# Dilated attention of the later queries: distant keys by residue class instead of densely

## Chip, core and metric

The kernel runs on one core of a Trainium2 chip, in one launch. The metric is the device time of the whole launch in microseconds, the median of the runs. Engines are named as the profile names them: PE (TensorE), PEld (its weight loads), DVE (VectorE), ACT (ScalarE), POOL (GpSimd) and SP, which issues the DMAs.

## What is computed

One decoder layer of 1024 tokens and width 1024: an input projection feeds eight heads of dilated attention (width 64 each) and four heads of a gated linear recurrence (HGRN2); both are normalised, joined by `w_out`, and followed by a squared-ReLU MLP. What matters here is the attention. It mixes three causal patterns, weighted by their softmax denominators:

```python
DILATED_PATTERNS = ((128, 1), (512, 4), (2048, 16))   # (window, dilation)
...
span = window // dilation
valid = (dist >= 0) & (dist <= span) & (blk * ATTN_BLOCK + kj - ATTN_BLOCK >= 0)
bias = -slopes[:, None, None] * (dist * dilation).astype(jnp.float32)
...
w = jax.nn.softmax(jnp.stack(lses, axis=0), axis=0)
o = jnp.sum(w[..., None] * jnp.stack(outs, axis=0), axis=0)
```

The mixture equals one softmax in which a key counts once for each pattern that holds it. A query at distance d sees every key with d <= 128, every key with d a multiple of 4 up to 512, and every key with d a multiple of 16. Beyond 128 tokens only keys of the query's own residue class modulo 4 can count.

## The kernel before

The stages follow one another: input normalisation and first projection, the recurrence heads (`hgrn_core`, four times), the attention, the output projection, the MLP. All matmuls are fp32; most operands are split into a high and a low part (`split_into`, `three_pass`), so that one product is two or three matmuls. The order on every engine is the order of the program (`manual_schedule`): each engine runs its instructions in the order in which they are written, and waits between engines are put in by data dependence. SP, too, issues its DMAs in that order, and waits in that order.

The attention works with blocks of 128 queries. For head `hd` and block `b` there is one step, 64 in all:

- `score` multiplies the block's queries with all keys up to the block's own end, `(b + 1) * 128` of them, in pieces of at most 512, once for the high and once for the low part of the keys. DVE adds the bias table (which holds the logarithm of the count, the ALiBi slope, and -1e30 where no pattern holds the key) and takes the maximum in the same instruction (L738).
- `expo` takes the exponential on ACT with the sum as by-product (L749).
- `turn` transposes the 128 x 128 blocks of the result on PE (L762), and ACT and DVE split them (L765, L766).
- `weigh` multiplies with the values for two blocks of queries at a time (`g = b // 2`, L779). The queries' high and low value halves come out as two halves of 64 rows.
- `finish` transposes back (L790), adds the halves (L794), and POOL multiplies by the reciprocal of the sums (L795).

The loop runs a pipeline by hand: in step s it issues the exponentials of step s + 1, the scores of step s + 2, the transposes of step s, the weighing of the pair of blocks before, and `finish` of the one before that. After these it takes work from `queue`, a list of generators (`fill`). A generator yields after each unit of about three matmuls. In the attention stage the queue holds the projections of the next pair of heads (`attn_proj`: 16 units each for queries, values and keys, 48 a pair), and later the first half of the output projection (`early_out`). `UNITS` says how many units follow each step; in the last 20 steps a budget of about 1000 ns does. `hooks` places single pieces of work, such as weight loads (`w_get`), at given steps.

`attn_proj` writes queries and keys of two heads into stacks and lets DMAs copy halves between partitions (L620, L621, L651, L652); `keys_off` and `keys_late` do this for the keys. `load_bias` loads one head's bias table of 1024 columns (L715). Tiles come from pools with tags: P (3 slots), S and T (9 each), BT and V8 (2 each), and PSUM banks `mm`, `s`, `t` and `pv` (2 each). A new tile waits for the readers of the one that held its slot.

Of the kernel before, what the change touches and what calls it, by code (L numbers as in the profile page):

```python
# [17 lines left out]
P = 128  # L18
# [9 lines left out]
LEVELS = (1, 2, 4, 8, 16, 32, 64)  # L28

# [6 lines left out]
def hymba_layer(ctx, tc, x, w_in, w_out, w_ff1, w_ff2, g_pre, lb_logits, g_mix, g_post,  # L36
# [406 lines left out]
    def hgrn_core(h, scale, after=None):  # L443
# [13 lines left out]
        if h < HH - 1:  # L457
            fill(1200 * scale)
            totals = slab("P", f"tot{h}")
            for step in range(3):  # L460
# [43 lines left out]
                cur = nx  # L504
                fill((7000, 7000, 7000)[step] * scale)
# [94 lines left out]
    pairs = [None] * (AH // 2)  # L600
    first_done = [False] * (AH // 2)
# [25 lines left out]

    def keys_early_read():
        pr, stacks, src, hf, _ = put_off.pop()
        put_off.append((pr, stacks, keys_read(pr, src, hf), hf, True))  # L630

    def attn_proj(pr):
# [79 lines left out]
    def load_bias(hd):  # L712
        if hd < AH and hd not in bts:
            bts[hd] = slab("BT", f"bt{hd}") if hd < AH - 1 else early["table"][:, 0]
            nc.sync.dma_start(out=bts[hd], in_=bias_tab[hd])  # L715

    def score(hd, b):
        stacks, _ = pairs[hd // 2]
        if b == 0:
            load_bias(hd)  # L720
            if hd + 1 < AH - 1:
                load_bias(hd + 1)
            stats[hd] = {n: tp.tile([P, NT, 2] if n == "mx" else [P, NT], F32, tag=n, name=f"{n}{hd}", bufs=2)
                         for n in ("mx", "nm", "dn", "rd")}
        q, kh, kl = (stacks[hd % 2][n] for n in ("q", "kh", "kl"))
        nk = (b + 1) * P
        mx, nm = stats[hd]["mx"], stats[hd]["nm"]
        pe = slab("P", f"p{hd}_{b}")
        pieces = []
        qs = q[:, b * P:(b + 1) * P]  # L730
        for pc in range(1 if nk <= 512 else 2):
            k0 = pc * 512
            n = min(512, nk - k0)
            pS = bank("s", f"ps{hd}_{b}_{pc}")
            TE.matmul(pS[:, :n], qs, kh[:, k0:k0 + n], start=True, stop=False)  # L735
            TE.matmul(pS[:, :n], qs, kl[:, k0:k0 + n], start=False, stop=True)  # L736
            o = 896 - b * P + k0
            V.tensor_tensor_reduce(out=pe[:, k0:k0 + n], in0=pS[:, :n], in1=bts[hd][:, o:o + n], scale=1.0,  # L738
                                   scalar=-3.0e38, op0=ALU.add, op1=ALU.max, accum_out=mx[:, b, pc:pc + 1])
            pieces.append((k0, n))  # L740
        if len(pieces) == 1:
            V.tensor_scalar(nm[:, b:b + 1], mx[:, b, 0:1], -1.0, None, op0=ALU.mult)  # L742
        else:
            V.tensor_scalar(nm[:, b:b + 1], mx[:, b, 0:1], mx[:, b, 1:2], -1.0, op0=ALU.max, op1=ALU.mult)
        return pe, nk

    def expo(hd, b, pe, nk):
        nm, dn = stats[hd]["nm"], stats[hd]["dn"]
        S.activation(pe[:, :nk], pe[:, :nk], AF.Exp, bias=nm[:, b:b + 1], accum_out=dn[:, b:b + 1])  # L749
        return pe  # L750

    def turn(hd, b, pe):
        g, u = divmod(b, 2)
        if u == 0:
            ns = (2 * g + 5) // 4
            pts[hd, g] = [[slab("T", f"pt{q}{hd}_{g}_{s}", F32R, (P, 4, 256)) for q in "hl"] for s in range(ns)]
        for s in range((b + 4) // 4):
            nj = min(4, b + 1 - 4 * s)
            pt = bank("t", f"pt{hd}_{b}_{s}")
            for j in range(nj):  # L760
                jj = s * 4 + j
                TE.transpose(pt[:, j * P:(j + 1) * P], pe[:, jj * P:(jj + 1) * P], ident)  # L762
            src = pt[:, :nj * P].rearrange("p (j c) -> p j c", j=nj)
            hi, lo = (q[:, :nj, u * P:(u + 1) * P] for q in pts[hd, g][s])
            S.activation(hi, src, AF.Copy)  # L765
            V.tensor_tensor(out=lo, in0=src, in1=f32(hi), op=ALU.subtract)  # L766
        dn, rd = stats[hd]["dn"], stats[hd]["rd"]
        V.reciprocal(rd[:, b:b + 1], dn[:, b:b + 1])

    def weigh(hd, g):  # L770
        _, vs = pairs[hd // 2]
        pt = pts.pop((hd, g))
        po = bank("pv", f"pov{hd}_{g}")
        nj = 2 * g + 2
        for j in range(nj):
            c0 = P if j == nj - 1 else 0
            vst = vs[:, j, hd % 2].rearrange("p a d -> p (a d)")
            for q in range(2):
                TE.matmul(po[:, c0:256], vst, pt[j // 4][q][:, j % 4, c0:],  # L779
                          start=j == 0 and q == 0, stop=j == nj - 1 and q == 1)  # L780
        ot = sp.tile([P, 256], F32, tag="ot", name=f"ot{hd}_{g}", bufs=1)
        S.activation(ot, po[:, :256], AF.Copy)
        return po, ot

    def finish(hd, g, po, ot):
        pr = hd // 2
        if anats[pr] is None:
            anats[pr] = slab("T", f"anat{pr}", F32, (P, NT, 2, 64))
        for u in range(2):
            TE.transpose(po[:, 256 + u * P:256 + (u + 1) * P], ot[:, u * P:(u + 1) * P], ident)  # L790
        pair = po[:, 256:].rearrange("p (u a d) -> p u a d", u=2, a=2)
        b = slice(2 * g, 2 * g + 2)
        dst = anats[pr][:, b, hd % 2]
        V.tensor_reduce(dst, pair.rearrange("p u a d -> p u d a"), axis=AX.X, op=ALU.add)  # L794
        G.tensor_tensor(out=dst, in0=dst, in1=stats[hd]["rd"][:, b].unsqueeze(2).to_broadcast([P, 2, 64]),  # L795
                        op=ALU.mult)
        if hd % 2 and g == NT // 2 - 1 and pr < AH // 2 - 1:
# [201 lines left out]
    steps = [(hd, b) for hd in range(AH) for b in range(NT)]  # L999
    scored, exped = {}, {}  # L1000

    def look(s):
        if s < len(steps):
            scored[s] = score(*steps[s])

    def raise_(s):
        if s < len(steps):
            exped[s] = expo(*steps[s], *scored.pop(s))

# [3 lines left out]
    def open_attention():  # L1013
        look(0)
        raise_(0)
        look(1)

    for h in range(HH):
# [11 lines left out]
        45: lambda: [drain(), keys_early_read(), row_turn(0, 0, tag="mm"), w_get(WO0 + 1, 0), row_rec(1)],  # L1030
        46: lambda: [keys_late(), early_sums(), queue.extend(early_out(t) for t in range(NE))],
# [13 lines left out]
    UNITS = ((3, 3, 3, 3, 2, 3, 1, 2), (4, 4, 4, 3, 2, 3, 1, 2), (4, 4, 4, 4, 3, 3, 2, 2))  # L1045
    n_steps = len(steps)
    to_weigh, to_fold = [], []
    for s in range(n_steps):
        if s % 16 == 6:
            first_done[s // 16] = True  # L1050
        hd, b = steps[s]
        ready, to_weigh = to_weigh, []
        raise_(s + 1)
        fresh = (s + 2) % 16 == 0
        if not fresh:
            look(s + 2)
        turn(hd, b, exped.pop(s))
        if b % 2:
            to_weigh.append((hd, b // 2))
        to_fold, last_fold = [(i, g, weigh(i, g)) for i, g in ready], to_fold  # L1060
        if fresh and s + 2 < n_steps:
# [927 lines left out]
```

## Time and profile before

| | |
|---|---|
| Median of 3 runs | 1231.17 us (1231.1 to 1232.23) |
| Span of the profiled execution (first to last instruction) | 1229.3 us |
| PE busy | 1220.1 us, 99% |
| DVE busy | 869.4 us, 71% |
| ACT busy | 546.9 us, 44% |
| POOL busy | 308.7 us, 25% |
| DMA, mean over the span | 130 GB/s, 38.5% of 16 engines for the main queue |
| First scores and last weighing of the attention | 302.3 us and 535.6 us |

The profile has no time of its own for the profiled execution beyond its span; the span is 1.9 us below the median of the runs. PE, PEld, DVE, ACT and POOL are engines; "busy" counts the time in which an instruction runs. Because matmuls are pipelined, a busy PE need not be at its peak: the distance between the starts of two matmuls says what one costs. A line such as L762 is a line of the kernel before. A row of groups reads: line, engine, operation, output<-inputs, shapes, count | busy us, mean ns | idle time before, and what ended it.

### The profile page before, as it was taken

The page shows a single profiled execution, that of the slowest core. Times are in us where ns is not written, and L with a number is a line of the kernel's source. Part 1 is how long each engine was busy: PE and PEld are TensorE (multiplying, and loading weights), DVE is VectorE, ACT ScalarE, POOL GpSimd, SP SyncE. Part 2 cuts the span into 40 slices and gives each one's busy share as a digit, 9 for nine tenths or more (in the row PEclk, how much of TensorE's full clock was granted, in tenths as well). Part 3 has the DMA queues.
Part 4 walks back from the last instruction along what each step waited for, and adds up shares of the span by engine and source line. Part 5 has one row for each costly group of instructions (what it writes and reads, how often), then busy time and mean ns, then how long its engine had stood idle before and what let it go on. Part 6 is the DMA issues. An engine that isn't in the chain of part 4 may idle for free.

```text
span 1229.3 us, 17165 instructions
## 1 busy us (share of the span) xinstructions
PE 1220.1 (99%) x6462; PEld 1047.5 (85%) x6462; DVE 869.4 (71%) x1498; ACT 546.9 (44%) x1003; POOL 308.7 (25%) x304
## 2 busy tenths in 40 slices
PE   9999999999999999999999999999999999999998
PEld 8898989888888888888888888888888888888886
DVE  5686969675766667768679667676678555488796
ACT  7633333223565557665575122222244353534562
POOL 0000000012222223246250676756622000000023
PEclk9999999999999999999999999999999999999999
DMA  5201111133232324254334446544487634433337
GB/s 215 70 18 52 35 52 35 35 86 86 70 88 67 86 69 140 78 196 145 117 125 146 171 180 223 194 183 164 153 311 273 238 103 154 155 103 88 119 102 275
DMA packets 61138, 159.75 MB, mean 130 GB/s; under 512 B 5248, under 2 KB 13184, under 8 KB 61056
## 3 DMA queue, kind: packets, MB, share of 16 engines
q1 hardware_dynamic: 61056, 158.66, 38.5%
q8 instruction: 51, 0.84, 0.3%
q14 instruction: 31, 0.25, 0.1%
HBM read 110.40 MB, written 41.94 MB: 124 GB/s over the span
## 4 chain that ended last, share of the span: by engine, by line
PE 96%; ACT 1%; DVE 1%; issue 0%; DMA 0%; POOL 0%; SPq 0%; DVEq 0%; POOLq 0%; ACTq 0%
PE f L1729 18%; PE f2s L1729 7%; PE pov L779 3%; PE pt L762 3%; PE pig L88 2%; PE pig L89 2%; PE pig L87 2%; PE pl L468 2%; PE pwo L87 2%; PE pwo L89 2%; PE pwo L88 2%; PE ps L736 1%; PE ps L735 1%; PE pm_av L87 1%; PE pm_ak L87 1%; PE pm_aq L87 1%
## 5 line engine op out<-in xcount | busy, mean ns | idle before, releaser
L84 DVE TENSOR_TENSOR al<-ar,ah 128x1024 fp32r<-128x1024 f32 x56 | 70.6, 1261 | 80.0 <-ACT ah L83 77.8
L1729 PE MATMUL f<-bh,ah 128*128 128x512 f32 x320 | 124.5, 389 | 0.0
L1729 PE MATMUL f<-bl,ah 128*128 128x512 f32 x320 | 124.5, 389 | 0.0
L1729 PE MATMUL f<-bh,al 128*128 128x512 f32 x320 | 124.5, 389 | 0.0
L83 ACT ACTIVATE ah<-ar 128x1024 fp32r<-128x1024 f32 x56 | 59.1, 1056 | 85.4 <-DMA ar<-actd 85.1
L1729 PEld LDWEIGHTS f<-bl,ah 128*128 128x128 f32 x320 | 60.1, 188 | 12.6
L1729 PEld LDWEIGHTS f<-bh,ah 128*128 128x128 f32 x320 | 60.1, 188 | 12.5
L1729 PEld LDWEIGHTS f<-bh,al 128*128 128x128 f32 x320 | 60.1, 188 | 12.3
L1803 POOL TENSOR_SCALAR lbl<-ssq 128x1 f32<-128x1 f32 x4 | 3.3, 821 | 245.7 <-ACT fd L1799 245.5
L766 DVE TENSOR_TENSOR ptl<-pt,pth 128x512 fp32r<-128x512 f32 (+2 forms) x96 | 50.3, 552 | 20.0 <-ACT pth L765 19.9
L765 ACT ACTIVATE pth<-pt 128x512 fp32r<-128x512 f32 (+2 forms) x96 | 43.3, 486 | 39.4 <-PE pt L762 38.1
L738 DVE CUSTOM_DVE_ANT_0 p<-ps,bt 128x512 f32<-128x512 f32 (+2 forms) x84 | 44.4, 554 | 21.8 <-PE ps L736 21.3
L1352 POOL TENSOR_TENSOR e<-x,e 128x512 f32<-128x512 f32 x14 | 21.6, 1543 | 131.0 <-DVE x L1303 131.0
L795 POOL TENSOR_TENSOR anat<-anat,rd 128x128 f32<-128x128 f32 x32 | 16.3, 510 | 147.2 <-DVE anat L794 144.9
L749 ACT ACTIVATE p<-p,nm 128x128 f32<-128x128 f32 (+3 forms) x64 | 49.5, 773 | 6.4 <-DVE nm L742 6.0
L79 POOL TENSOR_SCALAR ms<-hss 128x8 f32<-128x8 f32 x4 | 0.8, 198 | 199.3 <-DVE hss L585 199.3
L1729 PE MATMUL f2s<-bh,al 128*128 128x512 f32 (+1 forms) x128 | 48.9, 382 | 0.0
L1729 PE MATMUL f2s<-bl,ah 128*128 128x512 f32 (+1 forms) x128 | 48.9, 382 | 0.0
L1729 PE MATMUL f2s<-bh,ah 128*128 128x512 f32 (+1 forms) x128 | 48.9, 382 | 0.0
L762 PE MATMUL pt<-ident,p 128*128 128x128 f32 x288 | 42.5, 274 | 0.3 <-DVE ptl L766 0.3
L84 DVE TENSOR_TENSOR bl<-br,bh 128x1024 fp32r<-128x1024 f32 x32 | 40.1, 1253 | 1.0 <-ACT bh L83 0.9
L779 PE MATMUL pov<-pth,v 128*128 128x256 f32 (+1 forms) x160 | 40.3, 287 | 0.0
(1645 smaller groups left out, 3936.3 us busy)
## 6 DMA issues: line engine op xcount, KB each, us to landing
ar<-actd SPq DMA_DIRECT2D x56, 512.0 KB, 3.7
br<-in_w_ff_dram SPq DMA_DIRECT2D x16, 1024.0 KB, 6.2
w1r<-in_w_ff_dram SPq DMA_DIRECT2D x14, 1024.0 KB, 6.4
raw<-in_w_in_dram SPq DMA_DIRECT2D x26, 512.0 KB, 3.6
actd<-e SPq DMA_DIRECT2D x17, 768.0 KB, 4.1
actd<-e SPq DMA_DIRECT2D x11, 1024.0 KB, 4.0
raw<-in_w_out_dram SPq DMA_DIRECT2D x8, 512.0 KB, 3.5
xres<-in_x_dram SPq DMA_DIRECT2D x8, 512.0 KB, 4.2
```

Source lines behind the costliest of these rows:

```text
L83: S.activation(hi, src, AF.Copy)
L84: eng.tensor_tensor(out=lo, in0=src, in1=f32(hi), op=ALU.subtract)
L87: TE.matmul(dst, lhs[0], rhs[0], start=start, stop=False)
L88: TE.matmul(dst, lhs[0], rhs[1], start=False, stop=False)
L89: TE.matmul(dst, lhs[1], rhs[0], start=False, stop=stop)
L738: V.tensor_tensor_reduce(out=pe[:, k0:k0 + n], in0=pS[:, :n], in1=bts[hd][:, o:o + n], scale=1.0, scalar=-3.0e38, op0=ALU.add, op1=ALU.max ...
L749: S.activation(pe[:, :nk], pe[:, :nk], AF.Exp, bias=nm[:, b:b + 1], accum_out=dn[:, b:b + 1])
L762: TE.transpose(pt[:, j * P:(j + 1) * P], pe[:, jj * P:(jj + 1) * P], ident)
L765: S.activation(hi, src, AF.Copy)
L766: V.tensor_tensor(out=lo, in0=src, in1=f32(hi), op=ALU.subtract)
L779: TE.matmul(po[:, c0:256], vst, pt[j // 4][q][:, j % 4, c0:], start=j == 0 and q == 0, stop=j == nj - 1 and q == 1)
L1729: TE.matmul(pm, a[:, j, c], b[:, j, d], start=start and j == 0 and q == 0, stop=stop and j == 1 and q == 2, skip_group_check=True)
```

## The change

Queries 0 to 511 (blocks 0 to 3) are computed as before and are now called kind D ("dense"). For queries 512 to 1023 the keys are divided in two:

- Kind N ("near"): for blocks 4 to 7 the own block and the one before, 256 keys, densely.
- Kind F ("far"): keys two or more blocks back. The 512 queries are taken by residue class modulo 4, four groups of 128, and each group meets only the 192 keys of its class among tokens 0 to 767. The far bias is -1e30 where a key is less than two blocks back.

A softmax over near and far keys needs a common maximum and a common sum. The near statistics lie by block (partition = token within the block), the far ones by class (partition = token divided by 4). They are brought into each other's order through small DRAM tiles (`swap_dram`): `send` writes 128 x 4 numbers and `receive` reads them in the other order. `joint` takes the larger of the two maxima. Three such exchanges are made per head: near maxima, far maxima, far sums.

Each head now has eight items: D0 to D3, F0, F1 (two classes each), N0, N1 (two blocks each). Far weighing uses values in the class's order, and near weighing adds to the same PSUM bank, which is laid out by class. For this, `attn_proj` writes a pair's values to DRAM, and `far_load` reads them back in rows of 96 keys. The far bias tables are made once during the first three recurrence heads: `far_table` reads every fourth row of each head's bias table, POOL picks every fourth column, and a DMA stores the result (`far_dram`). `load_bias` loads 512 columns of the old table and 192 of the far one.

The order of the loop is written out anew (`ITEMS`, `LOOKS`, `UNITS`), `keys_late` is called once per pair, at step 13 of 16, and the next pair's projections are queued at step 14 of 16.

The core of the diff (allocation of tiles, and bodies that only carry over the old code to kind D, are cut):

```diff
+DIL = 4
+FAR = 192
+FC = FAR // 2
...
                 cur = nx
+                far_table()
                 fill((7000, 7000, 7000)[step] * scale)
...
+    def far_load(pr):
+        fars[pr] = []
+        for c in range(2):
+            t = slab("T", f"vf{pr}_{c}", F32R, (P, DIL, 2, 2, 64))
+            nc.sync.dma_start(out=f32(t[:FC]).rearrange("p r h a d -> p (r h a d)"),
+                              in_=v_dram[pr][c * FC * DIL:(c + 1) * FC * DIL].rearrange("(k r) c -> k (r c)", r=DIL))
+            fars[pr].append(t)
...
+    def far_table():
...
+        for b in range(4, NT):
+            w = (b - 1) * P
+            g = slice((b - 4) * 32, (b - 3) * 32)
+            nc.sync.dma_start(out=raw[g, :w],
+                              in_=bias_tab[hd].rearrange("(i r) c -> i r c", r=DIL)[:, 0, 896 - b * P:896 - b * P + w])
+        G.tensor_copy(far_box["out"][:, hd % 4],
+                      raw[:, :FAR * DIL].rearrange("p (k r) -> p k r", r=DIL)[:, :, 0])
...
+                if n == 6 and hf == 0:
+                    nc.sync.dma_start(out=v_dram[pr].rearrange("(n p) c -> p n c", p=P),
+                                      in_=f32(vs).rearrange("p n h a d -> p n (h a d)"))
+                    if pr == 0:
+                        far_load(0)
...
+    def look(hd, kind, g):
...
+        if kind == "D":
+            b = g
+            jobs = [(q[:, b * P:(b + 1) * P], lambda k: k[:, :(b + 1) * P], st["D"][b], bt[:, 384 - b * P:512], b)]
+        elif kind == "N":
+            jobs = [(q[:, b * P:(b + 1) * P], lambda k, b=b: k[:, (b - 1) * P:(b + 1) * P], st["N"][:, b - 4],
+                     bt[:, 256:512], b) for b in range(4 + 2 * g, 6 + 2 * g)]
         else:
+            jobs = [(q.rearrange("p (m r) -> p r m", r=DIL)[:, r, P:], lambda k, r=r:
+                     k.rearrange("p (m r) -> p r m", r=DIL)[:, r, :FAR], st["F"][:, r], bt[:, 512:512 + FAR], 8 + r)
+                    for r in range(2 * g, 2 * g + 2)]
+        o = 0
+        for qs, keys, dst, bias, i in jobs:
+            n = dst.shape[-1]
+            TE.matmul(pS[:, o:o + n], qs, keys(kh), start=True, stop=False)
+            TE.matmul(pS[:, o:o + n], qs, keys(kl), start=False, stop=True)
+            V.tensor_tensor_reduce(out=dst, in0=pS[:, o:o + n], in1=bias, scale=1.0,
+                                   scalar=-3.0e38, op0=ALU.add, op1=ALU.max, accum_out=mx[:, i:i + 1])
+            o += n
...
+    def tokens(ap, far):
+        flat_ = ap.rearrange("m r -> (m r)")
+        return flat_.rearrange("(m r) -> m r", r=DIL) if far else flat_.rearrange("(b p) -> p b", p=P)
+
+    def send(hd, i):
+        st = stats[hd]
+        src, far = ((st["mx"][:, 8:12], True), (st["mx"][:, 4:8], False), (st["dn"][:, 8:12], True))[i]
+        nc.sync.dma_start(out=tokens(swap_dram[hd][i], far), in_=src)
+
+    def receive(hd, i):
+        dst, far = ((stats[hd]["xf"], False), (stats[hd]["xn"], True), (stats[hd]["xd"], False))[i]
+        nc.sync.dma_start(out=dst, in_=tokens(swap_dram[hd][i], far))
+
+    def joint(hd, i):
+        st = stats[hd]
+        sl, other = ((slice(4, 8), "xf"), (slice(8, 12), "xn"))[i]
+        V.tensor_tensor(out=st["nm"][:, sl], in0=st["mx"][:, sl], in1=st[other], op=ALU.max)
+        V.tensor_scalar(st["nm"][:, sl], st["nm"][:, sl], -1.0, None, op0=ALU.mult)
...
+            for r in range(2 * g, 2 * g + 2):
+                for c in range(2):
+                    for q in range(2):
+                        TE.matmul(po[:, r], v_of(fars[hd // 2][c], r)[:FC], pt[q][:FC, 2 * r + c],
+                                  start=r == 0 and c == 0 and q == 0, stop=False, skip_group_check=True)
+            return None
+        po = stats[hd]["po"].rearrange("p (r m) -> p r m", r=DIL)
+        for j, s0, n, c0 in (((3, 0, 1, 0), (4, 1, 2, 0)), ((5, 3, 2, 1), (6, 5, 2, 2), (7, 7, 1, 3)))[g]:
             for q in range(2):
+                TE.matmul(po[:, :, c0 * 32:(c0 + n) * 32], v_of(vs, j),
+                          pt[q][:, :, s0:s0 + n].rearrange("p r s i -> p r (s i)"),
+                          start=False, stop=j == 7 and q == 1, skip_group_check=True)
...
-    UNITS = ((3, 3, 3, 3, 2, 3, 1, 2), (4, 4, 4, 3, 2, 3, 1, 2), (4, 4, 4, 4, 3, 3, 2, 2))
+    UNITS = ((2, 3, 4, 3, 2, 2, 2, 2), (3, 3, 4, 4, 3, 2, 2, 2), (3, 4, 4, 4, 3, 2, 3, 3))
+    ITEMS = (("D", 0), ("D", 1), ("D", 2), ("D", 3), ("F", 0), ("F", 1), ("N", 0), ("N", 1))
+    LOOKS = {0: ((0, "D", 2), (0, "N", 1)), 1: ((0, "D", 3), (0, "F", 0)), 2: ((0, "F", 1),),
+             6: ((1, "D", 0),), 7: ((1, "D", 1),)}
...
+        if i in (3, 5):
+            joint(hd, 1 if i == 3 else 0)
+        raise_(*((hd, *ITEMS[i + 1]) if i < 7 else (hd + 1, *ITEMS[0])))
+        if s % 16 == 13 and s < n_steps - 16:
+            while not put_off:
                 fill(1.0)
+            keys_late()
...
+        if i == 0:
+            send(hd, 1)
+        elif i == 1:
+            receive(hd, 1)
+        elif i == 2:
+            send(hd, 0)
+        elif i == 3:
+            receive(hd, 0)
+        elif i == 5:
+            send(hd, 2)
+        elif i == 6:
+            receive(hd, 2)
+        if s % 16 == 15 and s < n_steps - 1:
+            far_load(s // 16 + 1)
...
+        if i == 7:
+            look(hd + 1, "N", 0)
```

In this loop `look` issues scores and maxima, `raise_` exponentials, `turn` transposes and splits, `weigh` and `finish` the rest, for one item each. The diff changes nothing in the recurrence's own arithmetic, the output projection or the MLP.

More of the change, by code (lines that the diff above doesn't have):

```diff
@@ L1048, in hymba_layer @@
     for s in range(n_steps):
[L1049 removed]
+        hd, i = divmod(s, 8)
+        if s % 16 == 3:
             first_done[s // 16] = True
[L1051 removed]
         ready, to_weigh = to_weigh, []
[L1053 to L1061, printed above, removed]
[L1062 to L1067 removed]
```

254 lines of the change are left out of this document (153 added, 101 removed).

## The prediction

> **What bounds the kernel now.** I read the page first, then the stretches of the attention stage, then the waits, and last the chain and TensorE's timeline, which give the prices.
>
> ```profile
> span 1229.3 us, 17165 instructions
> ...
> PE 1220.1 (99%) x6462; PEld 1047.5 (85%) x6462; DVE 869.4 (71%) x1498; ACT 546.9 (44%) x1003; POOL 308.7 (25%) x304
> ...
> PE 96%; ACT 1%; DVE 1%; issue 0%; DMA 0%; POOL 0%; SPq 0%; DVEq 0%; POOLq 0%; ACTq 0%
> ...
> 299.80:512.00 212.20, 212.20 (x1288) 186.54 (x1287) 146.07 (x452) 125.83 (x282) 51.75 (x58) 1.00 0.33 93
> 512.00:540.00 28.00, 27.71 (x170) 23.79 (x169) 20.46 (x53) 20.36 (x47) 8.91 (x18) 1.00 0.23 67
> ...
> PE pt L762 <- DVE ptl L766: 0.3, 1, 0.3
> ```
>
> The two long rows are the attention stage: length, then busy time of PE, weight loads, DVE, ACT and POOL, the granted clock, the share of the DMA engines and GB/s. TensorE never stops (212.20 of 212.20 us) and has its full clock (1.00); VectorE works 69% of the time and ScalarE 59%. Its largest wait in this stage is 0.3 us, and 96% of the chain is TensorE. So the stage is as long as the sum of TensorE's instructions, counted from one start to the next (a record's own duration overlaps the next). Work taken from TensorE shortens the kernel one to one while the queue of projection matmuls is filled into the same steps. What DVE and ACT save is worth nothing; what they lose in waiting counts once TensorE runs out of cover.
>
> The span is 1229.3 us and the median of the three runs 1231.17, so 1.9 us lie outside the instructions or between executions. I subtract from the span and carry the 1.9 us along.
>
> **TensorE's prices.** One head now, blocks 4 to 7 (chain, then timeline: start, duration, instruction):
>
> ```profile
> 376.99 0.55 PE pt L762 x5
> ...
> 380.79 0.66 PE pt L762 x6
> 383.90 0.79 PE pt L762 x7
> 384.69 1.38 PE pov L779 x12
> ...
> 387.05 0.88 PE pt L762 x8
> 389.98 1.86 PE pov L779 x16
> ...
> 430.20 0.39 PE L735 MATMUL ps<-kh,q 128*128 128x512 f32 x1
> ...
> 430.65 0.22 PE L735 MATMUL ps<-kh,q 128*128 128x128 f32 x1
> ...
> 430.82 0.52 PE L762 MATMUL pt<-ident,p 128*128 128x128 f32 x3
> ...
> 434.84 0.28 PE L735 MATMUL ps<-kh,q 128*128 128x256 f32 x1
> ...
> 435.07 0.60 PE L762 MATMUL pt<-ident,p 128*128 128x128 f32 x4
> ...
> 438.92 0.33 PE L735 MATMUL ps<-kh,q 128*128 128x384 f32 x1
> ...
> 439.26 0.71 PE L762 MATMUL pt<-ident,p 128*128 128x128 f32 x5
> ```
>
> A pair of score matmuls (kh, kl) costs 0.45 us for 512 keys (430.20 to 430.65), 0.17 for 128, 0.23 for 256 and 0.34 for 384. A transpose costs 0.11 (0.88 / 8), a weighing matmul over 256 queries 0.116 (1.86 / 16). The 128-wide pair is two matmuls of 0.085, but eight transposes in a row, also 128 wide and each with its own weight load, cost 0.11 each; in a long run of short matmuls I take 0.11.
>
> Removed per head (blocks 4 to 7, keys up to the own block):
> - scores: four pairs of 512 and one each of 128, 256, 384 and 512: 4 x 0.45 + 1.19 = 2.99 us
> - transposes, 26: 0.55 + 0.66 + 0.79 + 0.88 = 2.88 us
> - weighing (g = 2, 3): 1.38 + 1.86 = 3.24 us
>
> Together 9.11 us.
>
> Added per head:
> - near scores (kind N), four pairs of 256: 4 x 0.23 = 0.92 us
> - far scores (F), four residues, pairs of 192 keys: between the 128 and the 256 pair; I take two of 0.11, so 4 x 0.22 = 0.88 us
> - transposes, 8 near and 8 far: 16 x 0.11 = 1.76 us
> - far weighing, 16 matmuls 128 wide: 0.085 to 0.11 each, 1.36 to 1.76; I take 1.76 us
> - near weighing, six of 256 and four of 128: 6 x 0.116 + 4 x 0.085 = 1.04 us
>
> Together 6.36 us. The eight transposes of the results stay. Saved: 9.11 - 6.36 = 2.75 us per head, **22.0 us for eight heads**. Blocks 0 to 3 (kind D) keep their instructions. The queued projection work is the same 48 units a pair, only dealt out differently (UNITS), so nothing moves in the sum.
>
> **The price no row shows.** Far queries and keys are read with one fp32 in four, 16 bytes apart. Nearest rows: the first and last of the seven levels of the recurrence (eight products of 64 queries, 16 records):
>
> ```profile
> 253.59 1.89 PE L529 MATMUL pl<-qt,kt 128*128 128x64 f32 x16
> 255.29 0.48 PE L87 MATMUL pm_aq<-hTh,wh 128*128 128x512 f32 x1
> ...
> 283.76 1.89 PE L529 MATMUL pl<-qt,kt 128*128 128x64 f32 x16
> 285.46 0.48 PE L87 MATMUL pm_ak<-hTh,wh 128*128 128x512 f32 x1
> ```
>
> The first reads every second fp32, the last 64 in a row, and both take 1.70 us. So a stride of 8 bytes is free for the moving operand here. For 16 bytes, and for weights, I take free too, because it is nearest to these rows. The other end is four times the price: a weight load of 4 x 0.11 us for each of eight matmuls is 3.5 us instead of 0.88, 2.6 per head, 21 us in all, which would eat the saving. Cheaper than contiguous is excluded, since no fewer elements are read. [...]
>
> **What hides the rest.** VectorE and ScalarE:
>
> ```profile
> L766 DVE TENSOR_TENSOR ptl<-pt,pth 128x512 fp32r<-128x512 f32 x48 | 32.4, 689 | 15.5 <-ACT pth L765 15.4
> ...
> L738 DVE CUSTOM_DVE_ANT_0 p<-ps,bt 128x512 f32<-128x512 f32 x42 | 28.4, 688 | 16.5 <-PE ps L736 16.1
> ...
> L738 DVE CUSTOM_DVE_ANT_0 p<-ps,bt 128x256 f32<-128x256 f32 x14 | 5.9, 420 | 2.5 <-PE ps L736 2.5
> ```
>
> Blocks 4 to 7 now need eight biased maxima and eight splits a head, four of each at 512. After, there are four maxima at 256 (0.42 us each), four at 192 (below that) and four splits at 512 (0.69): VectorE loses some 3 us a head and gains about 1 us of tiny joint operations. ScalarE trades four wide exponentials for eight narrow ones and copies half as much. Neither becomes the bound at 69% and 59%.
>
> The far table (40 small DMAs and eight POOL copies, most of a microsecond each) lies in the first three recurrence heads. POOL's later rsqrt is queued behind these copies, but POOL has little else there. The v spill (1 MB) and its reload (0.8 MB) per pair are read five steps later. I cost these at nothing; if a load lands late, the first far weighing waits and TensorE with it, a few us per pair at most.
>
> **The new wait.** Per head three statistics go out to DRAM and back in token order. `joint` waits on two of them, VectorE first; behind it are queued the split for the next weighing, and on ScalarE the far or near exponentials. Rows for small transfers (KB each, median us from issue to landing; then SP's waits in us, times, longest) and for the stage's length:
>
> ```profile
> q<-ql SPq DMA_DIRECT2D x16, 128.0 KB, 2.2
> ...
> gpre<-in_g_pre_dram SPq DMA_DIRECT2D x1, 4.0 KB, 2.6
> ...
> lbl<-in_lb_logits_dram SPq DMA_DIRECT2D x1, 4.0 KB, 8.9
> ...
> SPq L651 <- POOL ql L650: 31.3, 8, 6.7
> ...
> L735 PEld LDWEIGHTS ps<-kh,q x96: 186/188/192, 302.3 to 522.3; 128*128 128x128 f32 x96
> ```
>
> Scores of step 0 begin at 302.3 and those of step 61 at about 522, 3.6 us a step; minus 22 / 64 that leaves 3.3. The near maxima are ready some 2.8 us into step 0 (scores after the weighing, then the maxima); `joint` for the far half stands at the head of step 3, so out and back have about 3 x 3.3 - 2.8 = 7 us, those of the far maxima 8 us. Two legs at 2.6 us are 5.2 us and fit; 4-byte pieces on one leg may add a microsecond. TensorE has its fill units as cover. Costs arise where a leg queues behind a big load or behind SP's wait for POOL, and in the last two heads, where fill is thinner and steps shorter (about 2.5 us). At 2.2 us a leg the 16 joints cost nothing; at 8.9 they cost far more than the saving. Nearest are the 2.2 and 2.6 rows. My estimate is 0.3 us of TensorE idle for each of 12 joints and 0.6 for the four of the last two heads, **6 us**.
>
> Sum: 1229.3 - 22.0 + 6.0 = 1213.3 us of span, 1215 us with the 1.9.
>
> **Rivals.**
> 1. The exchange binds. SP runs in order: a `receive` waits for its `send`, and both stand behind weight loads and query copies, which SP has waited up to 6.7 us for (row above). If out and back take 9.5 us instead of 5.2, each joint is 2.5 us late and all 16 cost 40 us: 1231 - 22 + 40 = 1249 us, slower. It decides from 22 / 16 = 1.4 us of TensorE idle per joint. For it: TensorE's queue is in order and the last heads have little fill. Against: DMA is 33% busy in this stage, and 16 copies of 128 KB land in 2.2 us.
> [...]
> 3. The change doesn't shorten TensorE's work, since fill takes its place: 1231 us. This needs the chain to be bound by VectorE or by latency instead; 96% PE speaks against it.
> 4. Short matmuls pack better and the exchange is free: far weighing 1.36 instead of 1.76 us a head and no idle, 1231 - 25 = 1206 us.
>
> **How the numbers follow.** Forecast case (1208 to 1222): 0.60. The exchange binding, slower: 0.18. The stride costing: 0.14, of which 0.12 stays faster and 0.02 doesn't. No change: 0.04. Better than forecast: 0.04. A difference of 0.2% (2.5 us) is about what a measurement of this kernel can tell from none. Faster: 0.60 + 0.12 + 0.04 = 0.76; same: 0.04; slower: 0.18 + 0.02 = 0.20. The likeliest case gives 1215. The range runs from 1206 (rival 4) to 1236 (the upper end of the stride); some 0.15 of the exchange's 0.18 lies above it and little below.
>
> **What would show it.** Right: in the attention stage TensorE still full but 16 us shorter, pairs of far scores starting 0.22 us apart, PE transposes 26 a head, and the waits of DVE for the exchanged maxima long without a wait of PE behind them. The exchange is to blame if PE waits on splits or exponentials for over 1.4 us at joints; the stride, if a far pair takes 0.4 us or more at full clock. I am wrong altogether if PE has no idle time and the stage isn't shorter, or if the time is lost outside 300 to 540 us, say by late tables or weights.

## The result

The kernel after takes 1294.8 us (median of 4, 1290.2 to 1298.6) against 1231.1 before on the same chip: 1.0514 times the time, 95% interval 1.0485 to 1.0543. Forecast were 1215 us and 1206 to 1236. The sign was wrong, and the time lies beyond the rival that was to make the kernel slower (1249).

The page of the kernel after, with the lines that answer to those of before:

```profile
span 1290.0 us, 17087 instructions
...
PE 1233.7 (96%) x6366; PEld 1047.0 (81%) x6366; DVE 844.8 (65%) x1426; ACT 534.7 (41%) x1027; POOL 310.9 (24%) x305
...
PE 84%; DMA 8%; DVE 4%; ACT 3%; issue 1%; SPq 0%; POOL 0%; DVEq 0%; POOLq 0%; ACTq 0%
```

The 96 instructions that should go from TensorE went. But DMA holds 8% of the chain that ended last, where it held none. The stretches of the attention stage (columns as before; the second is a piece of the first):

```profile
299.80:575.00 275.20, 231.78 (x1251) 192.40 (x1251) 128.36 (x411) 117.49 (x308) 50.74 (x52) 0.97 0.41 88
540.00:560.00 20.00, 12.73 (x75) 11.20 (x74) 6.29 (x19) 8.44 (x27) 0.80 (x2) 0.83 0.39 116
```

TensorE, full in this stage before, is idle for 43 of 275 us, and its clock is below 1.00 for a part of it. Four periods of 3.4 or 6.8 us at half clock add up to 20.5 us; before there was none.

For a sum I took each TensorE instruction from its start to the next start, set aside gaps above 30 ns as idle, and added up by what the instruction works on, over the whole execution (us). The sums lie 7.6 to 8.1 below the spans in every column, so the columns can be compared. The last row leaves out the fall of the clock at the very end of every execution:

| | before | after | e1 | e6 | e7 | e4 | e12 |
|---|---|---|---|---|---|---|---|
| scores | 34.7 | 43.7 | 35.1 | 34.6 | 34.6 | 26.5 | 30.6 |
| transposes | 29.4 | 24.3 | 25.7 | 21.8 | 20.7 | 19.9 | 19.8 |
| weighing | 38.7 | 42.8 | 48.3 | 41.1 | 39.8 | 38.9 | 38.5 |
| folds of the results | 4.6 | 5.9 | 5.9 | 5.9 | 5.8 | 5.7 | 5.7 |
| projections | 229.9 | 230.6 | 235.9 | 229.1 | 229.9 | 228.9 | 228.8 |
| output product | 96.5 | 99.6 | 99.6 | 98.3 | 97.8 | 96.6 | 96.6 |
| the rest | 786.0 | 786.7 | 786.5 | 786.4 | 785.5 | 786.1 | 786.9 |
| idle | 1.8 | 48.4 | 43.1 | 15.8 | 8.1 | 8.7 | 6.6 |
| at half clock | 0 | 20.5 | 64.9 | 10.2 | 10.2 | 0 | 0 |

Each column is one profiled execution; for e4 and for e12 it is the quickest of the kernel's, at a mean granted clock of 0.999, and the slowest of either had 0.995, which in e10 goes with 10.2 us at half clock, so the zeros need not hold for their medians.

Two things stand out in the column of after: 46.6 us more idle time, and scores that cost 9.0 us more instead of 9.5 less. Three causes can be seen.

**The exchange.** The chain in the stage (start, duration, what), at the first head and at the third:

```profile
311.56 0.42 DVE pn L799
312.02 9.73 DMA swd<-stat
321.81 4.04 DMA stat<-swd
325.94 0.44 DVE stat L821
326.63 0.33 issue
326.97 0.62 ACT pf L835 x3
...
378.07 11.40 DMA swd<-stat
389.53 4.56 DMA stat<-swd
```

From the last near maximum (311.56) to the joint one (325.94) pass 14 us. 9.73 of them is the near maxima's way to DRAM. Over the eight heads this send takes 8.7 to 11.4 us. It writes 512 pieces of 4 bytes, because a partition's four statistics belong to four blocks. Who waits (us in total, times, longest; SP first, then the joint and the exponentials behind it):

```profile
SPq L816 <- DMA swd<-stat: 76.4, 19, 9.9
...
DVE stat L821 <- DMA stat<-swd: 32.3, 6, 7.2
...
ACT pf L835 <- DVE stat L822: 29.2, 7, 6.9
```

**The order inside a look.** TensorE's waits in the same view:

```profile
PE ps_F L797 <- DVE stat L799: 12.2, 16, 1.2
PE ps_N L797 <- DVE stat L799: 10.6, 16, 2.1
PE pt_F L856 <- DVE ptl L865: 7.3, 1, 7.3
PE pt_F L856 <- ACT pf L835: 5.2, 4, 2.9
```

All 32 near and far looks make TensorE wait in their middle, 22.8 us together. The timeline of one of them (start, duration, instruction, idle before it):

```profile
381.35 0.34 DVE L799 CUSTOM_DVE_ANT_0 pf<-ps_F,bt 128x192 f32<-128x192 f32 x1
381.61 0.08 DVE L799 DVE_READ_ACCUMULATOR2_ANT stat<- 128x1 f32 x1
381.74 0.31 PEld L797 LDWEIGHTS ps_F<-kh,q 128*128 128x128 f32 x1 [1.15 <-DVE stat L799]
381.75 0.55 PE L797 MATMUL ps_F<-kh,q 128*128 128x192 f32 x1 [0.91 <-DVE stat L799]
...
382.11 0.42 PE L798 MATMUL ps_F<-kl,q 128*128 128x192 f32 x1
...
382.35 0.62 PE L920 MATMUL pov_far<-ident,pn 128*128 128x128 f32 x4
```

The loop in `look` issues a job's two matmuls and its maximum, then the second job's into the other columns of the same PSUM tile, and the second job's matmul waits on VectorE's semaphore for the first job's maximum. Before, a piece had a bank of its own. Here two groups share one, and the 32 waits last 0.71 us on the average.

**The stride.** The pair that follows the wait takes 0.60 us (381.75 to 382.35) where 0.22 was assumed, and its weight load 0.31 us instead of the 188 ns of before. A part of the 0.60 belongs to the wait: in e7 below, without the wait, the 32 far pairs take 15.4 us, 0.48 each.

### The profile page after: what moved, and what is told of

The parts are those of the page before. It is cut to its first block, busy times and chain, and to the rows that moved or that the text cites. A ratio compares the mean times of both kernels' runs of the same rounds, so it can differ in the third digit from the quotient of the medians.

```text
span 1290.0 us, 17087 instructions
## 1 busy us (share of the span) xinstructions
PE 1233.7 (96%) x6366; PEld 1047.0 (81%) x6366; DVE 844.8 (65%) x1426; ACT 534.7 (41%) x1027; POOL 310.9 (24%) x305
## 4 chain that ended last, share of the span: by engine, by line
PE 84%; DMA 8%; DVE 4%; ACT 3%; issue 1%; SPq 0%; POOL 0%; DVEq 0%; POOLq 0%; ACTq 0%
PE f L1870 17%; PE f2s L1870 7%; DMA swd<-stat 4%; DMA stat<-swd 2%; PE pig L92 2%; PE pig L90 2%; PE pig L91 2%; PE pl L471 2%; PE pwo L90 2%; PE pwo L91 2%; PE pwo L92 2%; PE pm_f L90 1%; PE pm_f L92 1%; PE pm_f L91 1%; PE pm_ak L90 1%
## 5 line engine op out<-in xcount | busy, mean ns | idle before, releaser
L1870 PEld LDWEIGHTS f<-bh,ah 128*128 128x128 f32 x320 | 60.1, 188 | 12.5
L925 POOL TENSOR_TENSOR anat<-anat,stat 128x128 f32<-128x128 f32 (+1 forms) x24 | 13.1, 544 | 183.8 <-DVE anat L924 165.0
L1887 ACT ACTIVATE acc<-f 128x512 f32<-128x512 f32 x28 | 16.8, 598 | 49.1 <-PE f L1870 49.1
L86 ACT ACTIVATE bh<-br 128x1024 fp32r<-128x1024 f32 x32 | 33.6, 1051 | 4.6 <-PE f L1870 2.9
L87 DVE TENSOR_TENSOR wl<-raw,wh 128x1024 fp32r<-128x1024 f32 x23 | 29.0, 1263 | 9.1 <-ACT wh L86 8.5
L864 ACT ACTIVATE pth<-pt_D 128x128 fp32r<-128x128 f32 (+3 forms) x32 | 13.8, 432 | 50.3 <-PE pt_D L845 50.3
L658 POOL TENSOR_TENSOR kl<-kf,kh 64x512 fp32r<-64x512 f32 x16 | 20.4, 1275 | 50.7 <-ACT kh L657 50.1
L865 DVE TENSOR_TENSOR ptFl<-pt_F,ptFh 96x512 fp32r<-96x512 f32 x16 | 11.0, 687 | 32.1 <-ACT ptFh L864 31.1
L90 PE MATMUL pwo<-woh,mt 128*128 128x512 f32 x80 | 31.6, 395 | 0.3 <-ACT esum L1032 0.3
```

The lines of the kernel that those rows point to most:

```text
L87: eng.tensor_tensor(out=lo, in0=src, in1=f32(hi), op=ALU.subtract)
L90: TE.matmul(dst, lhs[0], rhs[0], start=start, stop=False)
L658: G.tensor_tensor(out=stacks[i]["kl"][a:b, sl], in0=full[a:b], in1=f32(stacks[i]["kh"][a:b, sl]), op=ALU.subtract)
L925: G.tensor_tensor(out=dst, in0=dst, in1=st["rd"][:, b].unsqueeze(2).to_broadcast([P, n, 64]), op=ALU.mult)
L1870: TE.matmul(pm, a[:, j, c], b[:, j, d], start=start and j == 0 and q == 0, stop=stop and j == 1 and q == 2, skip_group_check=True)
L1887: S.activation(acc_at(p, i), pm, AF.Copy)
```

## Experiments

Labels e1 to e12; all were timed against the kernel before on the same chip. Times are medians, ratios are to before with their 95% intervals.

### One cause at a time

**e1: in a look, all matmuls ahead of the maxima.**

```diff
             TE.matmul(pS[:, o:o + n], qs, keys(kl), start=False, stop=True)
+            o += n
+        o = 0
+        for qs, keys, dst, bias, i in jobs:
+            n = dst.shape[-1]
             V.tensor_tensor_reduce(out=dst, in0=pS[:, o:o + n], ...
```

> Edit: in a look of two jobs (N or F) the four matmuls are issued first and the two biased maxima after them; nothing else differs. Theory 'bank': in the changed kernel the second job's matmuls wait for the first job's maximum because both jobs write one PSUM bank (32 waits, 22.8 us of recorded TensorE idle, plus the refilling of the array after each); so without it the time falls by 20 to 35 us, to 1260 to 1275 us, and the waits of ps_F and ps_N for the maxima are gone. Rival 'exchange': TensorE would wait for the exchanged maxima anyway and the idle only moves to the transposes and weighing of the far keys; the time stays above 1285 us.

Measured: 1289.6 us, 1.046 (1.0427 to 1.0493), 5 us less than after, with intervals that overlap. The waits for the maxima are gone although the two jobs still share a tile, so the order of issue alone decides them. Scores fall by 8.6 us, which is all that shows of the refilling that the expectation names, but the time comes back elsewhere, as the waits of this kernel show:

```profile
PE pt_F L860 <- ACT pf L839: 20.0, 6, 5.6
PE pt_F L860 <- DVE ptl L869: 9.9, 1, 9.9
```

TensorE reaches the far transposes earlier and waits there for the exponentials and once for a split, both queued behind the joint maximum: 29.9 us instead of 12.5. The clock does the rest: 64.9 us at half clock instead of 20.5. So the rival was right for this edit alone.

**e2: no exchange of the maxima.** `joint` takes the own maxima, and the first two sends and receives go. So near and far weights no longer share a reference, and a part of the computation is left out.

```diff
-        V.tensor_tensor(out=st["nm"][:, sl], in0=st["mx"][:, sl], in1=st[other], op=ALU.max)
+        V.tensor_tensor(out=st["nm"][:, sl], in0=st["mx"][:, sl], in1=st["mx"][:, sl], op=ALU.max)
...
-        if i == 0:
-            send(hd, 1)
-        elif i == 1:
-            receive(hd, 1)
-        elif i == 2:
-            send(hd, 0)
-        elif i == 3:
-            receive(hd, 0)
-        elif i == 5:
+        if i == 5:
             send(hd, 2)
```

> Edit: near and far keys each take their own maximum; the two exchanges of maxima (sends, receives) are left out, that of the sums stays. So the common maximum is left out of the computation. Theory 'exchange': the leg that writes the near maxima to DRAM in 4-byte pieces takes 8.7 to 11.4 us and makes joint late in every head, by 3 to 7 us, which costs some 20 us of recorded waits on the far transposes and weighing and some 8 us of half clock after long stalls; the time falls by 25 to 40 us, to 1255 to 1270 us, and the granted clock is 1.00 throughout. Rival 'bank': joint's lateness is covered by queued projection work; the time falls by less than 10 us.

Measured: 1265.6 us, 1.0277 (1.026 to 1.0293): 29 us less, where expected. The clock of 1.00 that was expected with it did not come: 17.1 us are still at half clock.

**e3: far queries and keys read without a stride.** The far scores are then those of other tokens.

```diff
-jobs = [(q.rearrange("p (m r) -> p r m", r=DIL)[:, r, P:], lambda k, r=r:
-         k.rearrange("p (m r) -> p r m", r=DIL)[:, r, :FAR], ...
+jobs = [(q[:, 4 * P + r * P:4 * P + (r + 1) * P], lambda k, r=r:
+         k[:, r * FAR:(r + 1) * FAR], ...
```

> Edit: the far scores read 128 queries and 192 keys that lie in a row instead of every fourth one, same sizes and count; so the far scores are those of other tokens. Theory 'stride': a pair of far scores takes 0.60 us with operands 16 bytes apart and 0.22 to 0.25 without, 8 x 4 pairs, so 11 to 13 us of TensorE work go; as TensorE is idle elsewhere in the stage, 5 to 13 us of them reach the time, 1282 to 1290 us. Rival 'other': the pair stays at 0.60 us because of what surrounds it (the wait between the pairs), and the time stays within 3 us of the changed kernel's 1294.8.

Measured: 1296.5 us, 1.0537 (1.0515 to 1.0558), no gain, which neither expectation had for shorter pairs. The far pairs did become shorter (far scores from 20.2 to 11.5 us, counted as above), but idle time rose from 48.4 to 55.8 and half clock from 20.5 to 51.2 us: here a shorter pair was only a longer wait.

**e4: e1, e2 and e3 together,** which leaves out what e2 and e3 leave out.

> Edit: the three edits of e1, e2 and e3 together (common maximum left out, far scores of other tokens). If the three causes 'bank', 'exchange' and 'stride' are all there is, TensorE is full again and the saving of 22 us that the prediction worked out appears: 1205 to 1215 us. If another cause is left (loads of the values, thin queue in the last heads), the time stays above 1225 us and the waits of TensorE name it.

Measured: 1222.3 us, 0.9942 (0.9922 to 0.9962), between the two expectations. One edit at a time gave 5, 29 and -2 us; together they give 72. Each hid behind the others. In this kernel the far scores look as the prediction had them, 0.11 us a matmul in a row (0.12 on the average of all 64):

```profile
391.75 0.34 PE L797 MATMUL ps_F<-kh,q 128*128 128x192 f32 x1
...
391.92 0.27 PE L798 MATMUL ps_F<-kl,q 128*128 128x192 f32 x1
...
392.03 0.27 PE L797 MATMUL ps_F<-kh,q 128*128 128x192 f32 x1
...
392.14 0.27 PE L798 MATMUL ps_F<-kl,q 128*128 128x192 f32 x1
...
392.25 0.60 PE L924 MATMUL pov_far<-ident,pn 128*128 128x128 f32 x4
```

It also shows what the new tiling is worth by itself, which is less than 22 us (below).

### What makes the exchange slow

**e5: the near maxima written in rows of 16 bytes,** and read back 4 bytes at a time, one DMA for each block.

```diff
     def send(hd, i):
...
+        if i == 1:
+            nc.sync.dma_start(out=swap_dram[hd][i], in_=src)
+            return
...
     def receive(hd, i):
...
+        if i == 1:
+            rows_ = swap_dram[hd][i].rearrange("(m r) b -> b m r", r=DIL)
+            for b in range(4):
+                nc.sync.dma_start(out=dst[32 * b:32 * (b + 1)], in_=rows_[b])
+            return
```

> Edit: the near maxima are written to DRAM in rows of 16 bytes (128 of them) and read back 4 bytes at a time, by four DMAs of 32 partitions, instead of written as 512 pieces of 4 bytes and read in rows; the far exchanges stay. Theory 'pieces': writing 4-byte pieces to DRAM is what makes that leg take 9 to 11 us, reading such pieces is cheap (the far maxima and sums already do it, 2 to 3 us); the leg falls to 2 to 5 us, joint comes on time, and the time falls to that of e2 (1265.6 us), 1262 to 1272. Rival 'order': the leg is slow because SP issues it behind other transfers or because the exchange as such is too slow for the steps; the time stays above 1282 us.

**e6: e5 with the order of e1.**

> Edit: e1 and e5 together; the whole computation is kept. If 'pieces' and 'bank' are the causes of the waits, only the price of the stride (12.6 us of TensorE work by the starts of the far scores, 20.2 against 7.6 us in e4) is left on top of e4's 1222.3: 1232 to 1242 us, about the time of the kernel before. Rival 'order': above 1255 us.

Measured: e5 1271.9 us, 1.0323 (1.0305 to 1.034); e6 1243.4 us, 1.0096 (1.0081 to 1.0111). The change of the pieces is worth 23 us, and 46 once the order is mended (e1 to e6). e5 came as expected; e6 lies just above its 1232 to 1242 and well below its rival. The small transfers (KB each, median us from issue to landing), of after and then of e5:

```profile
swd<-stat SPq DMA_DIRECT2D x24, 2.0 KB, 3.9
stat<-swd SPq DMA_DIRECT2D x24, 2.0 KB, 3.2
```

```profile
stat<-swd SPq DMA_DIRECT2D x32, 0.5 KB, 2.1
swd<-stat SPq DMA_DIRECT2D x24, 2.0 KB, 2.1
stat<-swd SPq DMA_DIRECT2D x16, 2.0 KB, 2.6
```

The median of after mixes the eight sends of near maxima (8.7 to 11.4 us) with sixteen in rows (1.4 to 5.3). In the lower rows all sends are in 16-byte rows (2.1 us), and all receives read 4 bytes at a time. The 16 receives of 512 such pieces take 2.6 us (median); the sends that wrote 512 took 8.7 to 11.4. So 512 pieces of 4 bytes are slow here when they are written to DRAM, and not when they are read. Why, no run here shows. The edit changes the receive too, but that leg gains nothing: the four receives of a head take 3.9 to 4.8 us together in e5, the single one of after 2.3 to 6.1. At the first head of e6 the send takes 4.29 us and the last of the four receives 2.00; from the start of the send to the last landing pass 8.3 us, where after had 13.8:

```profile
311.93 4.29 DMA swd<-stat
318.26 2.00 DMA stat<-swd
```

### Which stride costs

**e8 and e9: e4 with only the queries (weights), and only the keys (moving), read without a stride.**

> Edit: e4 with only the far queries (the stationary operand) read in a row, the far keys every fourth one as in the change; common maximum left out and far scores of other tokens, as in e4. If the stride costs in the weight load, the far pair takes 0.22 us as in e4 and the time is 1222; if it costs in the moving operand, the pair takes 0.6 us and the time is 1233 to 1236.

> Edit: the reverse of e8: e4 with only the far keys (the moving operand) read in a row, the far queries every fourth one. If the stride costs in the weight load: pair 0.6 us and 1233 to 1236 us; if in the moving operand: 0.22 us and 1222 us. If both cost, e8 and e9 lie between, and their extra costs over e4 need not add, since a load runs beside the matmul before.

Measured: e8 1230.3 us, 0.9992 (0.9982 to 1.0003); e9 1231.4 us, 1.0002 (0.9992 to 1.0013). Both times lie between the 1222 and the 1233 to 1236 us of one cause alone: both strides cost, and the kernels take 8.0 and 9.1 us more than e4. TensorE's timeline, far pairs of e8 (keys strided), of e9 (queries strided) and of e7 below (both):

```profile
393.88 0.37 PE L798 MATMUL ps_F<-kl,q 128*128 128x192 f32 x1
394.05 0.37 PE L797 MATMUL ps_F<-kh,q 128*128 128x192 f32 x1
394.23 0.37 PE L798 MATMUL ps_F<-kl,q 128*128 128x192 f32 x1
```

```profile
394.53 0.39 PE L798 MATMUL ps_F<-kl,q 128*128 128x192 f32 x1
394.76 0.40 PE L797 MATMUL ps_F<-kh,q 128*128 128x192 f32 x1
395.00 0.40 PE L798 MATMUL ps_F<-kl,q 128*128 128x192 f32 x1
```

```profile
394.85 0.42 PE L798 MATMUL ps_F<-kl,q 128*128 128x192 f32 x1
395.08 0.42 PE L797 MATMUL ps_F<-kh,q 128*128 128x192 f32 x1
395.32 0.42 PE L798 MATMUL ps_F<-kl,q 128*128 128x192 f32 x1
```

From one start to the next, on the average of all 64 matmuls: 0.12 us with neither stride (e4), 0.18 with strided keys, 0.23 with strided queries, 0.24 with both. The far scores take 4.1, 7.0 and 7.8 us more than in e4, so the two prices don't add. The weight loads (ns: shortest, median, longest), of e4 and then of e9:

```profile
L797 PEld LDWEIGHTS ps_F<-kh,q x32: 186/190/192, 309.7 to 505.6; 128*128 128x128 f32 x32
```

```profile
L797 PEld LDWEIGHTS ps_F<-kh,q x32: 308/320/333, 309.7 to 516.5; 128*128 128x128 f32 x32
```

How load and stream share the time is not shown, since a load is recorded as longer than the distance between two matmuls. Not all of the 8.0 and 9.1 us is the stride: the profiled executions lie 9.1 and 12.8 us above e4's, and beside the 4.1 and 7.0 us of longer far scores they have 10.2 and 13.7 us at half clock, of which e4's has none. Why the clock drops in one and not in the other is open. The kernel e12 below also reads its keys at a stride, with far scores as long as e8's, and takes only 2.6 us more than e4. So with one fp32 used of each 16 bytes either operand is slower here: the far scores take 0.06 us a matmul more with strided keys and 0.11 more with strided queries.

### Keeping the whole computation

**e7: e1, and the constant 0 as the reference of the near and far exponentials.**

```diff
-        V.tensor_tensor(out=st["nm"][:, sl], in0=st["mx"][:, sl], in1=st[other], op=ALU.max)
-        V.tensor_scalar(st["nm"][:, sl], st["nm"][:, sl], -1.0, None, op0=ALU.mult)
+        V.memset(st["nm"][:, sl], 0.0)
```

The first two sends and receives go as in e2.

> In the looks of two jobs all four matmuls stand ahead of both maxima, and the near and far exponentials take the constant 0 for their reference instead of the joint maximum; so no maximum is exchanged, and the weights are still those of the reference after division by the sums, which are exchanged as before. Both far operands are read at a stride of 16 bytes. Theory of three separate costs: this is the 1222.3 us of the kernel without all three, plus what the two strides cost together, between the larger of the two costs measured one at a time (9 us) and their sum (17): 1231 to 1239. Rival, that the shared references are not what is left of the 1243.4 us of the kernel with the sends in rows of 16 bytes: 1241 or more.

Measured: 1233.6 us, 1.0019 (1.0009 to 1.0028), as expected. The costs now stand in a row, one step each: after 1294.8; order 5.2 less (e1, 1289.6); pieces 46.2 (e6, 1243.4); what is left of the exchange of maxima 9.7 (e7, 1233.6); strides 11.3 (e4, 1222.3), a step in which the constant also gives way to the own maxima. In another order the shares differ, as e1 to e3 showed.

**e10: e7, and the far queries copied into class order by ScalarE. e11: e6 with the same copies.**

```diff
+        for r in range(2 * g, 2 * g + 2):
+            t = classed[hd, r] = sp.tile([P, P], F32R, tag="cls", ..., bufs=2)
+            S.activation(t, q[:, r, P:], AF.Copy)
...
-            jobs = [(q.rearrange("p (m r) -> p r m", r=DIL)[:, r, P:], ...
+            jobs = [(classed[hd, r], ...
...
+        if i == 2:
+            class_order(hd, 1)
...
         if i == 7:
             look(hd + 1, "N", 0)
+            class_order(hd + 1, 0)
```

The second far look stands behind the transposes of its step, and `ot` of blocks 0 to 3 takes the place of old probabilities, which makes room for the copies.

> The kernel with the constant reference, and the far queries of each class copied by ScalarE into a contiguous tile of 128 columns ahead of the far looks (4 copies for each head, two of them behind the first far look, with the second far look moved behind the transposes of its step); the keys keep their stride. Theory, that the stationary stride costs by itself and ScalarE has room: 6 to 9 us below the kernel without the copies, 1225 to 1231. Rival, that the copies delay the exponentials and splits by as much as they save: within 2 us of the kernel without them.

> The whole exchange of maxima and sums is kept, the near maxima sent in rows of 16 bytes, all four matmuls of a look ahead of both maxima, and the far queries copied into class order as in the kernel beside it. Theory: 6 to 9 us below the 1243.4 us measured without the copies, 1234 to 1238. Rival, that the time left there is the wait for the references, so that quicker far pairs only lengthen it: 1241 to 1244.

Measured: e10 1232.3 us, 1.0008 (1.0 to 1.0017); e11 1247.2 us, 1.0131 (1.0113 to 1.0149). Neither gains: e10 lies 1.3 us below e7, with intervals that overlap, inside its rival's 2 us, and e11 3.8 above e6, beyond its rival's 1241 to 1244. The reasons that the rivals gave are not what the traces show. The far scores are 3.4 us shorter in both; the idle time ahead of the far transposes and the weighing is as in e7 (e10), or no longer than in e6 (e11). But TensorE waits for the copies, 4.6 us in both, and e11 has 20.5 us at half clock where e6 has 10.2 (waits, then timeline of e10):

```profile
PE ps_F L807 <- ACT cls L781: 4.6, 4, 1.7
```

```profile
371.57 1.28 ACT L686 ACTIVATE q<-qf 64x512 fp32r<-64x512 f32 x2 [2.73 <-DVE qf L683]
...
372.88 0.72 ACT L848 ACTIVATE pd<-pd,stat 128x512 f32<-128x512 f32 x1
...
373.60 0.73 ACT L781 ACTIVATE cls<-q 128x128 fp32r<-128x128 f32 x2
...
374.06 0.42 PE L807 MATMUL ps_F<-kh,cls 128*128 128x192 f32 x1 [1.67 <-ACT cls L781]
```

The copies of the second look stand in ScalarE's queue behind a projection's copy and an exponential.

**e12: those copies issued right behind the first far look.**

```diff
-        if i == 2:
-            class_order(hd, 1)
...
         for d, kind, g in looks[1:]:
             look(hd + d, kind, g)
+        if i == 1:
+            class_order(hd, 1)
```

> The kernel with the constant reference and the far queries copied into class order, with one move: ScalarE's copies for the second far look are issued right behind the first far look instead of a step later, behind an exponential and a projection's copy, where TensorE waited 4.6 us for them in four places (up to 1.7 us). Theory, that the 3.4 us saved in the far pairs were spent in those waits and the half clock behind them: 3 to 6 us less than the 1232.3 us with the later copies, 1226 to 1229, below the kernel before (1231.1). Rival, that ScalarE, now waiting for the first look's matmuls, delays other splits by as much: 1231 to 1233.

Measured: 1224.9 us (1223.3 to 1228.3), 0.9958 (0.9944 to 0.9972): 7.4 us less than e10, more than the 3 to 6 expected, and 0.4% less than the kernel before. Its page and its stage:

```profile
span 1221.5 us, 17071 instructions
...
PE 1207.3 (99%) x6366; PEld 1034.2 (85%) x6366; DVE 838.1 (69%) x1410; ACT 545.4 (45%) x1059; POOL 310.0 (25%) x305
```

```profile
299.80:512.00 212.20, 207.58 (x1256) 181.03 (x1255) 121.92 (x399) 130.41 (x347) 50.79 (x52) 1.00 0.41 114
```

Idle time is 6.6 us, where e10 has 12.1, and this execution, the quickest of the five, has none of the 10.2 us at half clock of e10's. With a constant reference the exponentials hold only while the scores stay in a range that exp can take in fp32. The earlier copies were not tried with the exchange kept (e11), nor were contiguous keys.

## Why the prediction was wrong

**What held.** TensorE set the stage, and the removed work was worth its time once nothing else came late: in e4 16.5 us less attention work and 6.9 us more idle time make 9.6 of the 10.1 us by which the profiled span fell. The transposes saved 9.5 us (29.4 to 19.9 in e4) of 9.0 forecast, the contiguous scores 8.2 of 9.5. VectorE and ScalarE did not become the bound (65% and 41% of the span). The spill of v and the far table cost nothing that shows: "the rest" and the projections are within 1 us of before.

**The exchange's legs, the step that failed.** The prediction took 2.6 us a leg, from copies of 128 KB and of 4 KB, and let "4-byte pieces on one leg" add "a microsecond", for which it had no row. That leg took 8.7 to 11.4 us, and out and back 14 to 16 at the two heads shown, against a room of 7. So the 6 us of idle time that the sum added became 46.6, with 20.5 us at half clock besides. Not all of it is the exchange's: the looks (below) hold 22.8 us. The prediction had the right size as the other end of a leg, a transfer of 4 KB that took 8.9 us. Its rival 1 priced 9.5 us out and back at 40 us, but got a chance of 0.18. Its own mark for it, 1.4 us of TensorE idle a joint, was just not reached: transposes and weighing show 13.9 + 7.1 us of idle time, 1.3 a joint. The experiments and not that mark show the cost: 29 us without the exchange of the maxima (e2), and 46 by the size of the pieces once the looks don't wait (e1 to e6).

**The wait in the middle of a look** was not foreseen. The prediction named `joint` as the only new wait. It priced a look as four matmuls in a row and didn't ask what stands between them: two jobs share a PSUM tile and the first one's maximum is issued ahead of the second one's matmuls. In the trace of after it is 22.8 us of waits, and 9.2 us in the products around them: near and far scores cost 32.8 us with the waits and 23.6 without (e1). Taken away alone it gave back 5 us, since the exchange was next.

**The stride as free** was the wrong end. It was taken from a stride of 8 bytes, in rows that could hardly show a price: their products of 64 columns started 0.106 us apart, as far as transposes of 128 columns do (0.11), so the columns seem not to have set their pace. The price of 16 bytes lies between the ends given, 0 and 21 us: 7.8 us in the far pairs, and 11.3 with what else changes from e7 to e4. The 1236 us at the upper end of the range stand on four times the price, an estimate of the author's that no run shows: from e4 to e7 a far matmul went from 0.12 to 0.24 us.

**Weighing.** 3.5 us of saving were forecast and none came (38.7 to 38.9 in e4). Far products, 128 wide, cost 0.125 us each there and near ones 0.134 on the average, where 0.11 and 0.085 to 0.116 were taken. There are 26 a head instead of 28, and the narrow ones were no cheaper than the 0.116 of before. The folds cost 1.1 us more, which the sum lacked. So the tiling is worth 16.5 us of TensorE's attention work (107.4 to 90.9 in e4), not 22.0.

**The idle time of 6 us** comes near the 6.9 us that e4 has more than before, but by luck: it was the price of 16 joints, and e4 exchanges no maxima. Rivals 3 and 4 had no part. Rival 1 and the case of a stride that costs were each right in kind; neither had the wait in the looks or the half clock, which the 1294.8 us also hold.

## What to carry to other kernels

When a transfer has no row of its own, price it by the size of its pieces and by whether it writes or reads them, not by its bytes; here 2 KB written in 512 pieces landed in 8.7 to 11.4 us, and 128 KB in 2.2 (median). In a run of matmuls on a full TensorE, ask of each one which semaphore it waits on: an eviction issued between two writers of one PSUM tile made TensorE wait 0.7 us each time here. When several causes sit one behind the other, single edits tell little: here 5, 29 and -2 us became 72.

## Not expected of the hardware

A DMA that writes 512 pieces of 4 bytes to DRAM landed in 8.7 to 11.4 us; one that reads 512 such pieces in 2.6 (median), and rows of 16 bytes were written in 2.1. TensorE's clock fell to half for 3.41 us or a multiple of it (20.5 us in all in after, 64.9 in e1, none in the profiled executions of before, e4 and e12), and within an execution all these periods begin on one grid of 3.41 us (in after 60, 69 and 79 steps of it behind the first one). They came without a long wait too: the shortest idle time in the 3.41 us ahead of such a period was 0.83 us (e10), and in e7, e8, e9 and e10 some began behind gaps of no more than 0.6 us each. But stretches of the grid with up to 1.67 us idle (after) passed without a fall, so what decides is open. The longest wait of after, 7.27 us up to 548.31, was paid twice, once as idle time and once in the products behind it: at the granted clock of 0.50 (548 to 552 us) matmuls of 512 columns started 0.43 us apart, and 0.23 at the full clock.
